# Delta rule in a two-layer trunk: decay differences by one product of masked rows, and row layouts of 1/rms by way of DRAM

## The chip, the cores and the metric

The kernel runs on one core of a Trainium2 chip. Five engines work from queues of their own: TensorE (PE: matrix products and transposes into PSUM), VectorE (DVE), ScalarE (ACT: activations, copies with scale), GpSimd (POOL) and SyncE (SP, which issues most DMAs). The metric is the device time of one execution in microseconds: the median of three runs is 2522.7 us (2521.9 to 2524.95).

## The reference

The program is a trunk of two layers over a sequence of 1024 tokens with 1024 channels. The even layer mixes a gated spatial part with a gated delta rule; the odd one is a differential attention. Each layer then has an MLP of 4096 channels and a gated embedding part (ple). Every part begins with an RMS norm, `x * rsqrt(mean(x*x) + eps) * gain`. What the change touches is the decay inside the delta rule, and the norms. Of the reference:

```
def l2_normalize(x):
    return x * lax.rsqrt(jnp.sum(x * x, axis=-1, keepdims=True) + NORM_EPS)

def chunk_gated_delta_rule(q, k, v, g, beta):
    ...
    gc = jnp.cumsum(g, axis=-1)
    causal = jnp.tril(jnp.ones((c, c), dtype=bool))
    strict = jnp.tril(jnp.ones((c, c), dtype=bool), k=-1)
    diff = gc[..., :, None] - gc[..., None, :]
    decay = jnp.where(causal, jnp.exp(jnp.where(causal, diff, 0.0)), 0.0)
    a = jnp.where(strict, jnp.einsum('bhnid,bhnjd->bhnij', k_beta, k) * decay, 0.0)
    u = solve(t_mat, v_beta)
    w = solve(t_mat, k_beta * jnp.exp(gc)[..., None])
    qk = jnp.einsum('bhnid,bhnjd->bhnij', q, k) * decay
```

For each chunk and each of four heads, `diff` is a square matrix of differences of running sums, and `decay` its masked exponential. The kernel works with eight chunks of 128 tokens (the result doesn't depend on the chunk's length).

## The kernel before

**Stages.** The tokens lie in two halves of 512. The x of the first half is loaded and transposed, then the input projection of the even layer begins, and from there on a long row of projection products fills TensorE: an fp32 value is split in a high and a low part (`hi`, `lo`, of type fp32r; ScalarE casts, VectorE subtracts), and three products with 512 columns each stand for one (`mm3`, tiles `mm`). These products are dealt out as fill: `pump(n)` emits the projection up to its unit n, and between two calls the code emits a piece of the delta rule. `FILLA` units are shared over the eight chunks' preparation, `FILLB` over the solver, `FILLC` and `FILLD` over what follows (`merge`, `prep`), `FILLS` over the eight steps of the recurrence. The class `Ordered` ties TensorE's instructions to that order with a lag of three slots; a code part in `high_priority` is put ahead of what else is ready by the scheduler that orders the other engines' queues. The times of the stages in the profile: decay and k times k of the eight chunks 100 to 141 us, the triangular solver from 147 us, its merge from 189 us, all beside projection products.

**The delta rule's preparation.** `gates()` forms the running sums of the gates for all chunks by four small products (`pg`, 128x32 for each kind), exponentiates them (`eg`), and keeps three forms of the sums: `gsum`, its negative `nsum`, and `gparts`, a high and a low part in fp32r. `spatial_weights()` transposes the spatial part's weights (`pws`). Then, for each chunk c, the generator `ahead(c)`:

- forms `pd`, the sums of the chunk laid out along the columns for each head: eight products of 128x128 (four heads, high and low part), a column of `gparts` broadcast as weights against an identity in fp32r (`identr`); `pd` lies in one of the two PSUM buffers with the tag `aux`;
- takes exponentials of 128x128 on ScalarE, head by head, with the negative or the positive sum of the row as bias: `ring` (the strict lower part, `am`) and `dec` (the causal part, `du`); POOL masks each with an `affine_select`;
- transposes k (`pk`), and gets its inverse length `rk` (`inverse_length`: a square of 512 columns on ScalarE, a reduction on VectorE, a power on POOL) and the scaled copy `kt`; the q of a chunk goes the same way in a later stage;
- multiplies k by itself (`pkk`, 128x128 for each head, fp32), also into an `aux` buffer, and VectorE multiplies it into `ring`;
- stores the diagonal blocks (`diag`) and the whole (`am_dram`) in DRAM by SP's queue.

`solve()` loads `diag` into `work` and inverts the small blocks on VectorE (the result is `dt`), and builds the larger inverse on TensorE with 32x32 pieces (`py`, `pz`).

**The row layouts of 1/rms.** `rms(half, ...)` computes 1/rms of 512 tokens as `r`, with the token along the partitions (128x4). Where a later step needs it along the columns, the same in all partitions, four products of `r`, broadcast as weights, with the identity bring it into a PSUM buffer (eight instructions in fp32, tile `aux`), and ScalarE copies it into `rb` (line 267). Nine places do this. Three of them matter here: the second half in `load_x`, the first half of the MLP's result (`take_hs(0)` in `mlp`) and the second half in `ple`, where `rms(1, sqs)` is called while the third gate product is emitted. The MLP runs twice, once per layer, and in the last layer nothing uses the rows of the first half's result.

## Time and profile before

| | |
|---|---|
| median of three runs | 2522.7 us |
| profiled execution | 2522.26 us, span 2520.5 us |
| TensorE busy | 2503.7 us (99%), granted clock 1.0 |
| VectorE, ScalarE, GpSimd busy | 1839.6 (73%), 1307.8 (52%), 258.2 us (10%) |
| DMA | 398.49 MB, mean 158 GB/s |

How to read the lines that follow. A row of a timeline has the start in us from the span's beginning, the length, the engine, the line of the kernel, the operation, the tiles it writes and reads (`out<-in`), and how many instructions it joins. Timelines and groups give an instruction's own duration, and neighbours on one engine overlap; the chain of the work that ended last gives each piece only the time by which it moves the end on (start, length, engine, tile, line). A row of the waits has engine, waiting tile and line, what it waited for, then the sum in us, the times, and the longest. A row of the windows has the window, its length, the busy time of PE, PEld (weight loads), DVE, ACT and POOL with their instructions, the granted clock, and the DMA share and rate. TensorE executes an fp32 product of small size in two passes, each of which is an instruction in the rows. A group's row has the line, the operation, shapes, the count, the busy time and the mean; a DMA's group ends with the size in KB and the median time from issue to landing.

### The profile page before, as it was taken

What the parts mean: (1) busy time and instruction counts of PE and PEld (TensorE: products, weight loads), DVE (VectorE), ACT (ScalarE), POOL (GpSimd) and SP (SyncE); (2) the same over time, 40 slices, a digit from 0 to 9 for tenths busy, and PEclk for the clock granted to TensorE, in tenths of its full rate; (3) what the DMA queues carried; (4) which work ended last, traced back from release to release, by engine and by line L of the source; (5) the groups of instructions that cost most, each with busy time, mean ns of one, the idle gap of its engine ahead of it and who ended that gap; (6) DMA issues with size and microseconds to landing.
All of it is one profiled execution on the core that took longest, in us unless ns stands there. A gap on an engine that the chain in (4) does not pass through costs nothing.

```text
span 2520.5 us, 39929 instructions
## 1 busy us (share of the span) xinstructions
PE 2503.7 (99%) x13982; PEld 2145.8 (85%) x13982; DVE 1839.6 (73%) x3664; ACT 1307.8 (52%) x2633; POOL 258.2 (10%) x227
## 2 busy tenths in 40 slices
PE   9999999999999999999999999999999999999999
PEld 7998998888888878888999999988788888888887
DVE  7868665696667787656577777786886677787586
ACT  6645473555555434544466666564654455445452
POOL 0210220000000000000433333310000000000000
PEclk9999999999999999999999999999999999999999
DMA  7464435466557756543211111147375558655651
GB/s 239 131 172 106 137 116 190 130 209 213 184 166 273 236 175 195 183 148 111 86 48 51 47 43 43 60 147 260 133 227 196 177 187 278 214 188 182 204 180 59
DMA packets 310482, 398.49 MB, mean 158 GB/s; under 512 B 43428, under 2 KB 179592, under 8 KB 310280
## 3 DMA queue, kind: packets, MB, share of 16 engines
q1 hardware_dynamic: 309720, 395.40, 49.1%
q8 instruction: 110, 1.80, 0.3%
q14 instruction: 92, 0.75, 0.1%
q10 hardware_dynamic: 560, 0.53, 0.1%
HBM read 289.40 MB, written 106.43 MB: 157 GB/s over the span
## 4 chain that ended last, share of the span: by engine, by line
PE 95%; DVE 2%; ACT 1%; DMA 1%; issue 0%; POOL 0%; ACTq 0%; DVEq 0%; POOLq 0%
PE mm L76 83%; PE po L76 3%; PE aux L76 2%; PE qk L76 2%; PE tr L79 2%; DVE lg L1020 0%; DMA guv<-uv_dram 0%; PE aux L79 0%; PE pkk L76 0%; PE pks L76 0%; PE pkq L76 0%; PE pd L76 0%; ACT t L1466 0%; DVE lg L1031 0%; ACT lg L1023 0%
## 5 line engine op out<-in xcount | busy, mean ns | idle before, releaser
L76 PE MATMUL mm<-g,w 128*128 128x512 f32 x2592 | 603.4, 394 | 1.1 <-ACT g L223 1.0
L223 ACT CAST w<-raw 128x512 fp32r<-128x512 f32 x598 | 365.7, 618 | 457.4 <-PE mm L76 388.5
L76 PEld LDWEIGHTS mm<-g,w 128*128 128x128 f32 x2592 | 486.0, 188 | 116.1 <-ACT g L223 1.4
L76 PE MATMUL mm<-hi,w 128*128 128x512 f32 x1728 | 554.0, 396 | 0.3 <-ACT hi L1230 0.3
L76 PE MATMUL mm<-w,hi 128*128 128x256 f32 (+2 forms) x2528 | 504.3, 295 | 0.0
L224 DVE TENSOR_TENSOR w<-raw,w 128x512 fp32r<-128x512 f32 x534 | 365.1, 690 | 179.9 <-ACT w L223 172.6
L76 PEld LDWEIGHTS mm<-w,hi 128*128 128x128 f32 x2528 | 400.6, 188 | 13.5
L76 PEld LDWEIGHTS mm<-hi,w 128*128 128x128 f32 x1728 | 324.2, 188 | 73.8 <-ACT hi L1230 0.7
L76 PE MATMUL mm<-w,lo 128*128 128x256 f32 (+2 forms) x1264 | 369.9, 293 | 0.0
L76 PE MATMUL mm<-lo,w 128*128 128x512 f32 x864 | 340.8, 395 | 0.9 <-DVE lo L1231 0.9
L76 PE MATMUL mm<-t,w 128*128 128x512 f32 x1152 | 270.9, 394 | 1.2 <-ACT w L223 1.2
L76 PEld LDWEIGHTS mm<-t,w 128*128 128x128 f32 x1152 | 216.2, 188 | 52.8 <-ACT w L223 1.6
L76 PEld LDWEIGHTS mm<-w,lo 128*128 128x128 f32 x1264 | 238.0, 188 | 5.3
L76 PEld LDWEIGHTS mm<-lo,w 128*128 128x128 f32 x864 | 162.4, 188 | 37.0 <-DVE lo L1231 1.4
L260 POOL TENSOR_TENSOR r<-ms,mhalf 128x4 f32<-128x4 f32 x12 | 13.3, 1109 | 1519.4 <-DVE ms L258 1492.5
L224 DVE TENSOR_TENSOR g<-graw,g 128x512 fp32r<-128x512 f32 x216 | 147.0, 684 | 8.7 <-DMA gd<-g 8.1
L223 ACT CAST g<-graw 128x512 fp32r<-128x512 f32 x216 | 132.7, 617 | 28.5 <-PE mm L76 7.7
L1023 ACT ACTIVATE lg<-lg,nm 128x128 f32<-128x128 f32 (+7 forms) x128 | 99.4, 777 | 81.9 <-DVE nm L1020 79.6
L350 ACT ACTIVATE g<-g 128x512 f32<-128x512 f32 x96 | 60.5, 631 | 116.1 <-DVE g L284 109.2
L1020 DVE CUSTOM_DVE_ANT_0 lg<-qk,al 128x512 f32<-128x512 f32 (+3 forms) x128 | 74.9, 589 | 38.7 <-PE qk L76 36.6
L224 POOL TENSOR_TENSOR w<-raw,w 128x512 fp32r<-128x512 f32 x64 | 84.2, 1339 | 111.0 <-ACT w L223 64.8
L76 PE MATMUL mm<-ohi,w 128*128 128x512 f32 x256 | 85.4, 400 | 0.6 <-ACT ohi L1077 0.4
(346 smaller groups left out, 3586.3 us busy)
## 6 DMA issues: line engine op xcount, KB each, us to landing
raw<-in_w_mlp_dram SPq DMA_DIRECT2D x352, 256.0 KB, 3.2
graw<-gd SPq DMA_DIRECT2D x224, 256.0 KB, 3.0
gd<-g SPq DMA_DIRECT2D x192, 256.0 KB, 3.2
raw<-in_w_ple_gate_dram SPq DMA_DIRECT2D x76, 256.0 KB, 3.3
acc<-h_dram SPq DMA_DIRECT2D x64, 256.0 KB, 4.6
keep<-in_w_mlp_dram SPq DMA_DIRECT2D x64, 256.0 KB, 4.2
raw<-in_w_in_e_dram SPq DMA_DIRECT2D x60, 256.0 KB, 3.8
h_dram<-acc SPq DMA_DIRECT2D x48, 256.0 KB, 3.0
```

Of the source, the lines that this page charges most:

```text
L76: self._next(self.engine.matmul(*a, **k))
L79: self._next(self.engine.transpose(*a, **k))
L223: self.nc.scalar.copy(hi, src)
L224: (lo_engine or self.nc.vector).tensor_tensor(lo, src, f32(hi), ALU.subtract)
L260: nc.gpsimd.tensor_tensor(r, ms, self.mhalf[:, 0:4], ALU.pow)
L350: nc.scalar.activation(g, src, AF.Relu)
L1020: nc.vector.tensor_tensor_reduce(out=lg[:, k0:k1], in0=ps[:, : k1 - k0], in1=al[:, u0 + k0 : u0 + k1], scale=-1.0, scalar=3.0e38 if c == 0 ...
L1023: nc.scalar.activation(lg[:, :n], lg[:, :n], AF.Exp, bias=nm[:, r, nch - 1 : nch], scale=-1.0, accum_out=me.sums[:, b, r : r + 1])
```

## The change

- `gparts`, `gsum`, `nsum` and `identr` go. In their place `gates()` puts the high and low parts of the sums side by side, transposes them once (`pgt`, 128x128), and builds two sets of rows: `own` (ones in the upper 64 rows, the sums in the lower) and `others` (the negative sums above, ones below; one copy for each head, with the rows of other heads set to zero). Both are in fp32r, in one large tile `sums`.
- For a chunk, ScalarE copies `own` with the rows of other chunks scaled to zero (a 128x128 mask copy), and a single product of 128x512 gives the differences of all four heads, `pd`, at once. The two exponentials then take 512 columns each, without a bias and with a scale of 1 and -1.
- `inverse_length` of `rk` squares head by head and lets ScalarE sum the squares (`accum_out`); VectorE's reduction stays for the other case.
- `rms` can send the rows by DRAM (`far`): a DMA writes `r` to a small DRAM tile `rd`, another broadcasts it to all partitions as `rb`. This is used in the three places named above; in the last layer's MLP the rows are not made at all.
- `gates()` is emitted with high priority, `FILLC` and `FILLD` go from 26 and 31 to 28 and 29.

```diff
-FILLA, FILLB, FILLC, FILLD = 62, 36, 26, 31
+FILLA, FILLB, FILLC, FILLD = 62, 36, 28, 29
...
-        self.identr = self.cp.tile([P, P], F32R, name="identr")
-        nc.vector.tensor_copy(self.identr, self.ident)
...
         rb = None
-        if rows:
+        if rows and far:
+            d = self.dp.tile([4, P], F32, name=self.nm("rd"))
+            nc.sync.dma_start(d.rearrange("t p -> p t"), r)
+            rb = self.sp.tile([P, HT], F32, tag=f"rb{half}", name=self.nm("rb"), bufs=1)
+            nc.sync.dma_start(rb, d.rearrange("t p -> (t p)").partition_broadcast(P))
+        elif rows:
             pb = self.aux_ps()
...
-        self.take_hs(0)
+        self.take_hs(0, rows=not last, far=True)
...
-                        rb[1] = self.rms(1, sqs)[1]
+                        rb[1] = self.rms(1, sqs, far=True)[1]
...
-            self.take_hs(half, ms)
+            self.take_hs(half, ms, far=half > 0)
...
-        gsum, nsum = carve([P, NC, G], 0), carve([P, NC, G], 0)
-        gparts = self.cp.tile([P, 2, NC, G], F32R, name="gparts")
+        in_any, in_chunk, in_head = carve([P, NC, G], 0), carve([P, NC, 1], 0), carve([P, G, 1], 0)
+        nc.vector.tensor_reduce(flat(in_any), self.ident.rearrange("p (q x) -> p x q", q=4), AX.X, ALU.add)
+        nc.vector.tensor_reduce(flat(in_chunk), in_any, AX.X, ALU.add)
+        nc.vector.tensor_reduce(flat(in_head), in_any.rearrange("p c h -> p h c"), AX.X, ALU.add)
+        own = carve([P, P], 0)
+        nc.vector.memset(own[0:64], 1.0)
...
-            nc.vector.tensor_copy(flat(gsum), pg[:, 0])
-            self.split(flat(gsum), flat(gparts[:, 0]), flat(gparts[:, 1]))
-            nc.vector.tensor_scalar(flat(nsum), pg[:, 0], -1.0, None, ALU.mult)
+            parts = self.tmp(P).rearrange("p (k q x) -> p k q x", k=2, q=2)
+            hi = hi_sums
+            nc.scalar.copy(hi, pg[:, 0])
+            for k in range(2):
+                nc.scalar.copy(parts[:, k, 0], f32(hi))
+                nc.vector.tensor_tensor(parts[:, k, 1], pg[:, 0], f32(hi), ALU.subtract)
+            pt = aux([P, P], "aux", "pgt")
+            self.pe.transpose(pt, parts.rearrange("p k q x -> p (k q x)"), self.ident)
+            nc.scalar.copy(own[64:P], pt[64:P])
+            other = self.tmp(P)
+            nc.vector.memset(other[64:P], 1.0)
+            nc.scalar.mul(other[0:64], pt[0:64], -1.0)
+            nc.vector.tensor_tensor(others, bc(other, G, 1), in_head.to_broadcast([P, G, P]), ALU.mult)
...
         def inverse_length(pt, name, sq):
-            nc.scalar.activation(sq, pt, AF.Square)
             l2 = self.sp.tile([P, G], F32, tag="l2", name=self.nm("l2"))
-            nc.vector.tensor_reduce(l2, sq, AX.X, ALU.add)
+            if name == "rk":
+                for h in range(G):
+                    nc.scalar.activation(sq[:, h], pt[:, h], AF.Square, accum_out=l2[:, h : h + 1])
+            else:
+                nc.scalar.activation(sq, pt, AF.Square)
+                nc.vector.tensor_reduce(l2, sq, AX.X, ALU.add)
...
+            w = sums[:, 1, (c % 4) * P : (c % 4 + 1) * P]
+            nc.scalar.activation(w, own, AF.Copy, scale=in_chunk[:, c])
             pd = aux([P, G, P], "aux", "pd")
-            for h in range(G):
-                for i in range(2):
-                    self.pe.matmul(pd[:, h], lhsT=gparts[:, i, c, h : h + 1].to_broadcast([P, P]), rhs=self.identr, start=i == 0, stop=i == 1)
-            for own, other in ((gsum, 1), (nsum, -1)):
+            self.pe.matmul(flat(pd), lhsT=w, rhs=flat(others), start=True, stop=True)
+            for other in (1, -1):
                 e = ring[:, c % 4] if other > 0 else self.slot(("c2", "c3", "c6", "d0")[c % 4], [P, G, P], F32, "dec")
-                for h in range(G):
-                    nc.scalar.activation(e[:, h], pd[:, h], AF.Exp, scale=-float(other), bias=own[:, c, h : h + 1])
+                nc.scalar.activation(e, pd, AF.Exp, scale=float(other))
...
-        gates()
+        sums = self.slot("A3", [P, 2, HT], F32R, "sums")
+        others = sums[:, 0].rearrange("p (h t) -> p h t", h=G)
+        with self.tc.high_priority(EARLY):
+            gates()
```

More of the change, by code (lines that the diff above doesn't have):

```diff
@@ L243, in add_square, with take_hs, rms @@
             nc.vector.tensor_tensor(self.sqs[half], self.sqs[half], sq, ALU.add)
-    def take_hs(self, half, ms=None, rows=True):
-        self.r[half], self.rb[half] = self.rms(half, self.sqs[half], ms, rows)
+    def take_hs(self, half, ms=None, rows=True, far=False):
+        self.r[half], self.rb[half] = self.rms(half, self.sqs[half], ms, rows, far)
         self.hs[half] = self.hs_new[half]
-    def rms(self, half, sqs, ms=None, rows=True):
+    def rms(self, half, sqs, ms=None, rows=True, far=False):
         nc = self.nc
@@ L1295, in even_mix @@
         nc.vector.memset(state, 0.0)
+        hi_sums = self.cp.tile([P, NC * G], F32R, name="hi_sums")
         def gates():
```

## The prediction

> **What bounds the kernel now.** I read the page first: the busy shares, the slices and the chain that ended last.
>
> ```profile
> span 2520.5 us, 39929 instructions
> PE 2503.7 (99%) x13982; PEld 2145.8 (85%) x13982; DVE 1839.6 (73%) x3664; ACT 1307.8 (52%) x2633; POOL 258.2 (10%) x227
> PEclk9999999999999999999999999999999999999999
> PE 95%; DVE 2%; ACT 1%; DMA 1%; issue 0%; POOL 0%; ACTq 0%; DVEq 0%; POOLq 0%
> ```
>
> TensorE is busy 99% of the span and is 95% of the chain, at its full clock in every slice. The waits say how much of the rest is waiting; their first row is the largest:
>
> ```profile
> PE tr L79 <- DVE olo L1078: 2.3, 3, 1.2
> ```
>
> So a TensorE instruction taken out shortens the program by its own length, as long as no new wait appears. Where one could, the share of VectorE matters, so I took the windows of the stretch in which the decay work runs (in each: PE, PEld, DVE, ACT, POOL):
>
> ```profile
> 100.00:120.00 20.00, 20.00 (x127) 17.61 (x126) 18.73 (x52) 13.61 (x42) 9.32 (x12) 1.00 0.51 158
> 120.00:140.00 20.00, 20.00 (x141) 18.42 (x140) 18.96 (x54) 13.72 (x42) 7.88 (x11) 1.00 0.68 190
> ```
>
> Here VectorE is at 94 to 95% and ScalarE at 68%: TensorE bounds, with VectorE just behind. The chain in this window (98 to 142 us) is TensorE alone, and its pieces give the advance per instruction without overlap:
>
> ```profile
> by line: PE mm L76 62.2%; PE pkk L76 16.9%; PE pd L76 15.1%; PE pk L79 6.0%
> ...
> 99.84 0.76 PE pk L79 x7
> ...
> 102.32 1.51 PE pd L76 x14
> 103.83 2.13 PE mm L76 x9
> ```
>
> pd is 15.1% of 44 us, 6.6 us for 64 instructions (0.108 each by the x14 row). A 128x512 product takes 2.13 / 9 = 0.237 us, a transpose 0.76 / 7 = 0.109 us.
>
> **The change, part by part.** (a) Eight products of 128x512 replace the 64: 8 x 0.237 = 1.9 us for 6.6, a gain of 4.7 us. (b) The row layout of 1/rms goes by DRAM in three places, and is dropped in one where nothing reads it.
>
> ```profile
> 61.02 0.89 PE aux L76 x8
> ...
> L76 PE MATMUL aux<-ident,r x72: 270/275/275, 23.7 to 2363.8; 128*128 128x128 f32 x72
> ```
>
> The 72 instructions are nine places of eight, and four of them go: 4 x 0.89 = 3.6 us of TensorE, with four ScalarE copies. (c) One transpose (pgt) is new: +0.1 us. (d) What TensorE now meets at the first chunks. On TensorE, where chunk 0 and 1 start (pd: decay differences, pkk: k times k, mm: input projection), before:
>
> ```order
> L76 MATMUL pd_1143<-identr,gparts 128x128 x7
> L76 MATMUL pd_1213<-identr,gparts 128x128 x7
> L76 MATMUL mm_1268<-hi_177,w_1129 128x512
> ...
> L76 MATMUL mm_1268<-hi_201,w_1190 128x512
> L79 MATMUL pk_1461<-ident,qkv_692 128x128
> L79 MATMUL pk_1540<-ident,qkv_692 128x128
> L76 MATMUL pkk_1254<-qkv_277 128x128 x4
> ```
>
> and after:
>
> ```order
> L76 MATMUL mm_1257<-hi_199,w_1189 128x512
> L76 MATMUL pd_1153<-sums_1046 128x512
> L76 MATMUL pd_1213<-sums_1046 128x512
> L79 MATMUL pk_1418<-ident,qkv_691 128x128
> L79 MATMUL pk_1487<-ident,qkv_691 128x128
> L76 MATMUL pkk_1243<-qkv_279 128x128 x4
> ```
>
> Nine projection products stood between the second pd and pkk; now none does. pkk takes the PSUM buffer of the first pd (two buffers turn), so it waits until both exponentials of chunk 0 are done. On ScalarE, for the same place, after (own and the other rows from pgt, then masks, squares, tanh, convolution copy, exponentials):
>
> ```order
> L1334 COPY carved_239<-pgt_1069 64x128
> L1337 ACTIVATE t_1072<-pgt_1069 64x128
> L1600 ACTIVATE sums_1046<-carved_239 128x128 x3
> L1580 ACTIVATE sq_1290,l_254_1291<-pk_1285 128x128 x4
> L1600 ACTIVATE sums_1046<-carved_239 128x128
> L1580 ACTIVATE sq_1359,l_266_1360<-pk_1354 128x128 x4
> L1386 ACTIVATE t_1129<-t_1124 128x512
> L1382 ACTIVATE t_1204<-cx_1201,cols 128x512
> L1605 ACTIVATE ring_1151<-pd_1153 128x512
> L1605 ACTIVATE dec_1157<-pd_1153 128x512
> ```
>
> All of these come after pgt and ahead of the release; before, only two squares of 128x512 stood between the tanh and the exponentials. Their prices (ScalarE, timelines):
>
> ```profile
> 103.09 1.14 ACT L1580 ACTIVATE ring<-pd,carved 128x128 f32<-128x128 f32 x4 [1.48 <-PE pd L76]
> 104.11 1.16 ACT L1580 ACTIVATE dec<-pd,carved 128x128 f32<-128x128 f32 x4
> ...
> 107.11 0.74 ACT L1365 ACTIVATE t<-t 128x512 f32<-128x512 f32 x1
> 107.64 0.83 ACT L1361 ACTIVATE t<-cx,cols 128x512 f32<-128x512 f32 x1
> ...
> 321.10 1.28 ACT L1797 ACTIVATE qkv<-qkv,fo 128x128 f32<-128x128 f32 x4 [2.87 <-DVE fo L1795]
> ...
> 323.29 0.40 ACT L1466 ACTIVATE t<-guv,mean 128x128 f32<-128x128 f32 x1
> 323.58 0.20 ACT L1466 ACTIVATION_READ_ACCUMULATOR t<-guv,mean 128x1 f32 x1
> 323.67 0.39 ACT L1466 ACTIVATE t<-guv,mean 128x128 f32<-128x128 f32 x1
> ```
>
> Back to back, a 128x128 exponential from PSUM advances (104.11 - 103.09) / 4 = 0.255 us, a scaled copy in SBUF 1.28 / 4 = 0.32, a 128x512 activation 0.53 (107.11 to 107.64), a summed square 0.38 with its read of the sum (323.29 to 323.67). That last one reads SBUF and has a pointer bias, which the new squares from PSUM have not; so they lie between 0.255, as if the sum were free, and 0.38. I take 0.28, nearer the exponential's row, since that reads PSUM too. The chain on ScalarE: two rows out of PSUM 0.5 (0.255 each at most), four masks 1.2 (the first is only part of a row ahead), eight squares 2.2, tanh 0.53, convolution copy 0.6, two exponentials 1.1: 6.1 us, with ends of 5.9 and 6.9. TensorE has, from pgt to pkk, 11 transposes (1.2), ten products (2.4), two pd (0.5) and two pk (0.2): 4.3 us. pkk therefore waits 6.1 + 0.3 for two handovers between engines (an estimate from the pd pieces: 102.32 + 1.51 ends where the next begins, so the trace shows none here; ends 0 and 0.6) - 4.3 = 2.1 us, within 1.6 and 3.2. pk_1418 waits for the tanh of the same row of work and lies inside that wait.
>
> The Trainium skill ("ScalarE: Activation LUTs", What ACT_TABLE_LOAD costs) says that every [128,1] pointer operand adds about 93 ns to an ACTIVATE. By that rule the summed square without its bias would be an estimated 0.38 - 0.093 = 0.29 us, and the wait about the same as mine; by the L1466 row as it stands it would be 0.8 us longer. No row here shows the same square with and without a pointer.
>
> (e) VectorE loses the reduction of rk (one of 128x512 per chunk) and gains a few in the idle start; ScalarE per chunk stays about equal: eight exponentials at 0.255 (2.0) and one square of 512 (0.5) become two of 0.53, four summed squares (1.1) and a mask (0.3), 2.5 against 2.5. So the later chunks cost nothing new; if that cover fails it is the third rival. The solver behind has room:
>
> ```profile
> 183.35 2.07 DVE L1647 STREAM_TRANSPOSE dt<-work 128x1024 f32<-128x1024 f32 x1
> ...
> 189.28 2.21 PE L76 MATMUL py<-dt,ay 32*32 32x32 f32 x128
> ```
>
> TensorE starts py 3.9 us after its input is there. It comes 0.9 (b) + 4.7 - 0.1 - 2.1 = 3.4 us earlier there, so even an unmoved solver would be in time by 0.5 us; the two fill units moved across it take nothing from the sum. (f) The DMA pairs: r is there (POOL) long before the rows are first read (DVE), and short transfers land within 5 us:
>
> ```profile
> 29.25 1.45 POOL L260 TENSOR_TENSOR r<-ms,mhalf 128x4 f32<-128x4 f32 x1 [7.82 <-DVE ms L841]
> 62.82 0.68 DVE L1357 TENSOR_TENSOR cx<-mm,rb 128x512 f32<-128x512 f32 x1
> ...
> 1025.01 1.01 POOL L260 TENSOR_TENSOR r<-ms,mhalf 128x4 f32<-128x4 f32 x1 [540.55 <-DVE ms L258]
> 1113.05 0.68 DVE L591 TENSOR_TENSOR t<-mm,rb 128x512 f32<-128x512 f32 x1
> ...
> 1120.47 1.01 POOL L260 TENSOR_TENSOR r<-ms,mhalf 128x4 f32<-128x4 f32 x1 [92.39 <-DVE ms L258]
> 1165.83 0.69 DVE L591 TENSOR_TENSOR t<-mm,rb 128x512 f32<-128x512 f32 x1 [0.23 <-PE mm L76]
> ...
> kg<-in_attn_k_gain_dram SPq DMA_DIRECT2D x2, 0.2 KB, 3.1
> ...
> vg<-in_gmlp_v_gain_dram SPq DMA_DIRECT2D x2, 256.0 KB, 3.9
> ```
>
> kg is 64 elements of four bytes, vg a row broadcast to all partitions: 3.1 + 3.9 = 7 us against 32, 87 and 44. In the first place SP issues other loads up to about 42 us, and the pair stands among them:
>
> ```profile
> 36.54 0.48 SPq L854 DMA_DIRECT2D kg<-in_attn_k_gain_dram  x1
> 41.91 0.97 SPq L101 DMA_DIRECT2D raw<-in_w_in_e_dram  x2
> ```
>
> The store of r comes right behind the first row and the broadcast ahead of the second, so it lands near 46, still 17 us early. What the pairs hold is SP's queue, where the broadcast waits for the store to land and later loads stand behind it. In the second place:
>
> ```profile
> 1025.12 0.43 SPq L324 DMA_DIRECT2D raw<-in_w_mlp_dram  x1
> 1029.25 0.32 SPq L324 DMA_DIRECT2D graw<-gd  x1
> ...
> 1038.08 0.62 ACT L223 CAST g<-graw 128x512 fp32r<-128x512 f32 x1
> ```
>
> SP idles from 1025.6 to 1029.25, about as long as r (1026.0) and kg's 3.1 us need; and with four buffers turning, the load of 1029.25 is read by the fourth cast after it, at 1038.08, landing (three us) some 5.8 us ahead. Cost 0.
>
> Sum: -4.7 - 3.6 + 0.1 + 2.1 = -6.1 us. The profiled execution took 2522.26 us (span 2520.5 and 1.8 around it), 0.4 under the median of 2522.7; so 2516.2 by its own time, 2516.6 by the median. I say 2516.8, for a few tenths of handovers.
>
> **Rivals.** A, likeliest: as summed, the wait between 1.6 and 3.2: 2515.9 to 2517.8. B, no wait: ScalarE's squares slip ahead of pgt, or the exponentials come in time: -8.2, 2514.5. For it: 99% busy; against it: the order above. C, the stretch from 99 to 140 turns into VectorE's and ScalarE's: VectorE is at 95% there, and chunks pass the same two buffers each time. TensorE's saving in it beyond the first two chunks is 6 x (0.84 - 0.24) = 3.6 us; it can give all of that back, plus up to 3 more if the solver ends as much later against its 0.5 us of room: 2518 to 2523. D, the slower one: SP. If a landing went by the number of elements, r's 512 would take 8 x 3.1 = 24.8 us, and the load behind it would come 21 us late at 1029; beyond 5.8 us of room TensorE stands for 15 us, net +9, 2532. It decides from 12 us of lateness on. Against it: vg moves 256 KB in 3.9. E, the clock: after a wait TensorE could be granted less.
>
> ```profile
> 0.00:4.00 4.00, 2.58 (x12) 2.53 (x12) 0.88 (x7) 1.49 (x2) 0.69 (x6) 1.00 0.53 107
> 4.00:8.00 4.00, 2.60 (x11) 1.59 (x10) 0.77 (x2) 1.26 (x3) 0.00 (x0) 1.00 0.99 325
> ```
>
> With idle gaps of 1.4 us in each of these the clock stays 1.00. If a longer wait halved it, the 15 products behind would take 0.47 instead of 0.237, +3.5 us: 2520.2. The Trainium skill ("TensorE: Matmul & The Clock Gate", What's actually happening) has such a rule: an idle window of about 3.4 us brings the array to half its clock until a busy one of that length has passed. By that rule the wait forecast here stays under the limit; its upper end is near it.
>
> **Chances.** A 0.50, B 0.10, C 0.26, D 0.08, E 0.06. A difference of 0.2% (5.0 us) is about the least that a measurement can tell here; faster means under 2517.7: A but for its upper end and B, 0.56; slower is D with the worst of C, 0.12; the rest, most of C and E, 0.32. The range leaves out D, the worst of C and the fastest of B: 2514.2 to 2521.8.
>
> **What would show it.** Eight pd of 128x512 near 0.24 us and 40 instead of 72 aux<-ident,r; one row in the waits, PE pkk or pk for ACT or DVE, of about 2 us near 104; full clock behind it; rb landing within 8 us of r. Wrong would make it: further pkk, pd or py rows in the waits (C), TensorE waiting for casts near 1035 or 1130 (D), or a pd row far above 0.24.

## The result: slower, and where the time went

The changed kernel takes 2531.8 us (seven runs, 2528.7 to 2533.7), the kernel before 2522.7 beside it: a ratio of 1.0031, with a 95% interval of 1.0020 to 1.0043. It is slower by 9.1 us, where 6.1 less were forecast. The profiled execution took 2533.74 us, at the upper end of its runs. From its page:

```profile
span 2532.0 us, 39755 instructions
PE 2499.9 (99%) x13895; PEld 2139.2 (84%) x13895; DVE 1838.6 (73%) x3660; ACT 1302.2 (51%) x2649; POOL 260.0 (10%) x227
PE 88%; DVE 4%; DMA 4%; ACT 2%; issue 1%; SPq 0%; POOL 0%; DVEq 0%; ACTq 0%; POOLq 0%
```

TensorE has 3.8 us less to do than before (2503.7), but its share of the chain falls from 95 to 88%: the chain now runs through DMAs and VectorE. The waits of TensorE in the changed kernel (before, the largest was 2.3 us in three pieces):

```profile
PE aux L79 <- DVE xt L815: 5.9, 1, 5.9
...
PE mm L76 <- DVE acc L288: 2.3, 2, 2.0
...
PE pk L79 <- DVE qkv L1387: 1.8, 1, 1.8
...
PE mm L76 <- DVE w L222: 1.7, 2, 1.5
PE mm L76 <- DVE t L1186: 1.6, 1, 1.6
...
PE py L76 <- DVE xts L1719: 1.3, 2, 1.1
```

The wait of 1.8 at `pk` is the one that was forecast. The first row is the large one, and it isn't in the decay part: it is a transposition of x (`aux`, line 79), which waits for VectorE to empty a PSUM buffer (`xt`). How it comes about is read from two queues. SyncE's timeline around the first of the three row layouts, changed kernel:

```profile
38.16 0.53 SPq L263 DMA_DIRECT2D rd<-r  x1
...
42.09 0.34 SPq L861 DMA_DIRECT2D sg<-in_attn_sub_gain_dram  x1
...
47.31 0.33 SPq L265 DMA_DIRECT2D rb<-rd  x1
```

The broadcast `rb` waits for the store `rd` to land: 47.31 - 38.16 = 9.1 us. Between them stands the load of `sg`, 128 single elements that only the attention of the second layer uses, more than 1000 us later. VectorE's timeline, changed kernel:

```profile
42.78 0.68 DVE L815 COPY xt<-aux 128x512 f32<-128x512 f32 x1
52.03 0.15 DVE L862 TENSOR_SCALAR sg<-sg 128x1 f32<-128x1 f32 x1 [8.57 <-DMA sg<-in_attn_sub_gain_dram]
...
53.42 0.68 DVE L815 COPY xt<-aux 128x512 f32<-128x512 f32 x1
```

and the same place in the kernel before:

```profile
41.68 0.15 DVE L858 TENSOR_SCALAR sg<-sg 128x1 f32<-128x1 f32 x1 [0.61 <-DMA sg<-in_attn_sub_gain_dram]
...
42.41 0.68 DVE L811 COPY xt<-aux 128x512 f32<-128x512 f32 x1
```

VectorE stood 0.61 us for `sg` before and stands 8.57 now. It takes its instructions in order, so the copies of x behind it are late by as much, and TensorE with them. Windows of the changed kernel (the last two numbers of a row are the DMA share and GB/s, the one ahead of them is the granted clock):

```profile
44.00:48.00 4.00, 4.00 (x21) 3.21 (x19) 0.00 (x0) 0.00 (x0) 0.00 (x0) 1.00 0.46 28
48.00:52.00 4.00, 0.32 (x2) 0.00 (x0) 0.00 (x0) 0.00 (x0) 0.00 (x0) 0.93 0.90 287
52.00:55.00 3.00, 0.75 (x5) 0.78 (x5) 2.97 (x7) 1.82 (x3) 0.00 (x0) 0.50 0.89 309
55.00:58.00 3.00, 3.00 (x10) 2.48 (x9) 2.96 (x6) 0.42 (x1) 0.00 (x0) 0.50 0.27 95
```

While the store is out, the other transfers crawl: 28 GB/s from 44 to 48 us. SyncE's queue stands from 43.5 to 47.3 us, until the store has landed, but that isn't all: transfers that it had issued from 39.4 to 43.0 us were out already, and those whose landing the trace gives took 10.0 to 10.6 us (`sg` 9.9 by VectorE's row, where the kernel before has 2.8). The stores of x, over the whole of the kernel before and then from 36 to 54 us in the changed one:

```profile
h_dram<-xt SPq DMA_DIRECT2D x16, 256.0 KB, 5.2
```

```profile
h_dram<-xt SPq DMA_DIRECT2D x3, 256.0 KB, 10.4
```

From 48 to 54 TensorE stands, and behind that it has half its clock until 58 us. That is rival E's clock, after another wait than the one it was priced for: 10 matmuls in the last 3 us, where 17 were done in the same window before:

```profile
55.00:58.00 3.00, 3.00 (x17) 2.54 (x16) 3.00 (x7) 2.49 (x6) 0.00 (x0) 1.00 0.08 14
```

How far TensorE stood behind the kernel before, place by place, worked out from the starts of the same instructions in the timelines (place named by its time before; the last column is the kernel of the first experiment, which has no far rows at the first place):

```
us before, what starts there            changed kernel   first place on TensorE
  45.6  third transposition of x            +0.7              +1.5
  55.4  fourth, its last instruction        +8.9              +1.5
  93.1  gates (pg)                          +8.3              +1.8
 189.3  solver (py)                         +6.4              -0.1
 203.4  merge (py of xts)                   +9.0              +1.3
 244.4  recurrence                          +7.8              +0.4
 307.4  recurrence                          +9.5              +0.7
1269.3  attention                           +7.1              -1.7
1751.8  output projection                   +8.9              -1.9
2256.3  MLP of the last layer              +12.5              -1.3
2516.4  end                                +11.5              -2.3
```

8.2 us are lost between the third and the fourth transposition (0.7 of them are three projection products that moved ahead of the fourth). From gates to solver 1.9 are gained, by the two other row layouts some 2.4 (9.5 to 7.1), by the dropped one 0.9. The four later waits take 1.3 (merge; the rest of that step is moved fill work, which the other kernel has too and gets back by 244), 1.7 (305), 1.8 (1745) and 3.6 (2237 us, with a halved clock). Profiles differ from that of the kernel before by up to 1.8 us at the start already, by when x arrives, so these columns are good to about that; totals are taken from medians.

### The profile page after: what moved, and what is told of

It reads as the page before. It is cut to its first block, busy times and chain, and to the rows that moved or that the text cites. A ratio compares the mean times of both kernels' runs of the same rounds, so it can differ in the third digit from the quotient of the medians.

```text
span 2532.0 us, 39755 instructions
## 1 busy us (share of the span) xinstructions
PE 2499.9 (99%) x13895; PEld 2139.2 (84%) x13895; DVE 1838.6 (73%) x3660; ACT 1302.2 (51%) x2649; POOL 260.0 (10%) x227
## 4 chain that ended last, share of the span: by engine, by line
PE 88%; DVE 4%; DMA 4%; ACT 2%; issue 1%; SPq 0%; POOL 0%; DVEq 0%; ACTq 0%; POOLq 0%
PE mm L76 77%; PE po L76 3%; PE qk L76 2%; PE aux L76 2%; PE tr L79 2%; DMA raw<-in_w_mlp_dram 1%; DMA guv<-uv_dram 1%; DVE t L1384 0%; DVE lg L1024 0%; DMA t<-h_dram 0%; DMA raw<-in_w_in_e_dram 0%; DMA sg<-in_attn_sub_gain_dram 0%; DVE w L222 0%; ACT junk L820 0%; PE pks L76 0%
```

## Experiments

Each time stands beside runs of the kernel before on the same chip. Two theories were tested first. S: the store of `r` at the first place is the loss, by the stand for `sg`. Rival C of the prediction: the decay part gives back what it gains and takes more.

**The first place back on TensorE.** Everything else of the change stays.

```diff
-            self.take_hs(half, ms, far=half > 0)
+            self.take_hs(half, ms)
```

> The changed kernel, with the row layout of load_x (the second half of x) back on TensorE; all else as changed. Theory 1 (the store of 512 four-byte elements holds the DMA rings for 8 to 9 us at 38 to 47 us; VectorE's queue stands at sg, whose load is behind it, TensorE stands 5.9 us and then runs at half its clock): the 8.2 us that TensorE lost between 45 and 58 us come back, less 0.9 for the eight products, so 2531.8 - 7.3 = 2524.5 us, and no wait above 2.5 us before 60 us. Theory 2 (the decay part's early reductions and the gates' priority make VectorE late at the start): the wait stays, 2532.7 us.

2520.97 us against 2522.42, ratio 0.9991 (0.9982 to 1.0000); 10.8 under the changed kernel's median. The 5.9 us row is gone, and so is the half clock from 52 to 58. The first two waits of this kernel:

```profile
PE tr L79 <- DVE olo L1082: 2.3, 3, 1.2
PE pk L79 <- DVE qkv L1387: 1.8, 1, 1.8
```

**The first place alone, in the kernel before.** `far` as in the change, used in `load_x` only.

> The kernel before, with the row layout of load_x (second half) by DRAM and nothing else changed. Theory 1: the same stand near 48 to 54 us and half a clock behind it, 2522.7 + 8.2 - 0.9 = 2530.0 us. Theory 2: 2522.7 - 0.9 = 2521.8 us.

2531.1 against 2522.4: 1.0032 (1.0019 to 1.0045), the loss of the whole change. Its waits have the same row, `sg` landed as late (VectorE stood 9.67 us), and the merge has its wait too:

```profile
PE aux L79 <- DVE xt L816: 5.7, 1, 5.7
...
PE py L76 <- issue: 1.8, 1, 1.8
```

So this line of the change, without any of the decay part, gives the result. That S is the cause of the loss and C isn't follows from these two runs together.

**All rows on TensorE; the decay part by itself.** The first is the kernel above with the other two far places back as well (the dropped rows stay dropped); the second has the old fill units (26, 31) and all rows, so it is the decay part alone.

> The changed kernel with all three row layouts back on TensorE; the one that nothing reads stays dropped, and the decay part is as changed. If the pairs in the MLP and in the ple part cost nothing but save their products (theory 1): 1.8 us above the kernel with only load_x back, 2526.3 us. If their stores cost time elsewhere too (a load that comes late in the MLP or the ple part): equal to it or below, 2522 to 2524.5 us.

> The decay part alone: all row layouts as before the change, the unused one too, FILLC and FILLD at 26 and 31. By the prediction's sum (a, c, d): 2522.5 - 4.7 + 0.1 + 2.1 = 2520.0 us. By the traces so far (a gain of 1.9 us from the gates to the solver): 2520.6 us. If the waits it sets off later eat it: 2522 to 2524 us.

2523.94 against 2522.42 (1.0004, 0.9995 to 1.0013), and 2523.34 against 2522.9 (1.0001, 0.9992 to 1.0010). By the first the second and third place are worth 3.0 us (2523.94 - 2520.97; forecast 1.8), but not all of that is their products: its profile has a wait of 2.2 us for `guv` near 387 us with a window at half clock behind it (388.8 to 392.2), where the kernel with only the first place back waits 0.9 at full clock. The second says that the decay part gains nothing that can be measured, where 2.5 were forecast. In its own stretch the gain is there; from the timeline of the decay part alone, first `pg` and first `py`, and the `pg` of the kernel before:

```profile
95.10 0.97 PE L76 MATMUL pg<-carved,carved 128*128 128x32 f32 x8
189.46 2.21 PE L76 MATMUL py<-dt,ay 32*32 32x32 f32 x128
```

```profile
93.06 0.97 PE L76 MATMUL pg<-carved,carved 128*128 128x32 f32 x8
```

Before it is 189.28 - 93.06 = 96.22 us from one to the other, now 94.36: 1.9 less. Up to 386 us the gain shrinks to 1.0 (a wait of 1.0 for `guv`, 0.6 before), and by 2256 us to 0.3, with a wait for `g` that the kernel before doesn't have (1.2 at 2230 in its own time).

**The rows part without the first place.** The kernel before with the second and third place far and the dropped rows.

```diff
-        self.take_hs(0)
+        self.take_hs(0, rows=not last, far=True)
...
-                        rb[1] = self.rms(1, sqs)[1]
+                        rb[1] = self.rms(1, sqs, far=True)[1]
```

> The kernel before with the row layouts of the MLP and the ple part by DRAM and the unused one dropped; load_x on TensorE, the decay part as before. If TensorE's saving there is whole (3 x 0.89 us) and the decay part is worth little once its waits are counted: 2522.5 - 2.7 = 2519.8 us, as fast as the kernel with the decay part and old fills (2520.2). If the decay part is worth its forecast 2.5 us beyond this: that kernel stays faster by 2 us, and this one stands at 2522 us.

2520.45 against 2522.9: 0.9991 (0.9982 to 1.0000), 2.45 us less; three times 0.89 is 2.7. Here the stores land just as slowly (9.1 us at 1025) and nobody waits for them.

**Is `sg` the only link?** In the changed kernel VectorE's instruction on `sg` is emitted at the start of the attention instead of the start of the program; the store stays as slow.

```diff
-        nc.vector.tensor_scalar(sg, sg, 1.0 - lam_init, None, ALU.mult)
...
+        self.pe.behind(nc.vector.tensor_scalar(self.sg, self.sg, self.sub, None, ALU.mult), self.pe.mark)
```

> The changed kernel (store of 512 elements in load_x kept), but VectorE's scaling of sg is issued only ahead of the attention, so that nothing on VectorE waits for sg at the start; its load stays where it is. Theory 1a (the slow load of sg, in order on VectorE, is the only link from the store to TensorE): no stand near 50 us, full clock, 2531.8 - 8.2 = 2523.6 us or a little less. Theory 1b (stores of x tiles and weight loads behind the slow store hold TensorE as well): a wait of 2 to 5 us stays between 45 and 60 us, 2527 to 2530 us.

2523.45 against 2523.5 (0.9998, 0.9989 to 1.0007). Its windows:

```profile
44.00:48.00 4.00, 4.00 (x23) 3.32 (x22) 3.96 (x9) 1.23 (x3) 0.00 (x0) 1.00 0.44 61
48.00:52.00 4.00, 4.00 (x20) 3.23 (x18) 2.84 (x7) 2.02 (x4) 0.00 (x0) 1.00 1.08 378
```

The transfers crawl as before (61 GB/s), `rb` is again issued 8.5 us behind `rd`, but TensorE works on at full clock. It lacks 1.8 us to the first experiment (0.9998 against 0.9991, intervals that overlap). Its profile, 2526.66 us and the slowest of its eleven runs, keeps the changed kernel's waits at the merge (1.3), at 1745 us (1.8, with a window at half clock behind it) and 2237 us (1.8). How much of the 1.8 each of them makes isn't shown.

**Another shape of the store.** `r` is first transposed on TensorE (one instruction), and four rows of 512 bytes are stored.

```diff
-            nc.sync.dma_start(d.rearrange("t p -> p t"), r)
+            pr = self.aux_ps()
+            self.pe.transpose(pr[0:4, 0:P], r, self.ident)
+            r4 = self.tmp(P)[0:4]
+            nc.scalar.copy(r4, pr[0:4, 0:P])
+            nc.sync.dma_start(d, r4)
```

> The changed kernel, but 1/rms is transposed to four rows on TensorE (one transpose of 128x4, a ScalarE copy) before the store, which then writes four rows of 512 bytes in place of 512 elements of four. Theory 1 (the elements' size is what holds the rings): the store lands within 3 to 4 us in place of 8 to 9, no stand near 50 us, 2531.8 - 8.2 + 0.3 = 2523.9 us. Theory 3 (any pair of a store and a broadcast at that place holds the loads of the start): 2529 to 2532 us.

2521.4 against 2522.4 (0.9996, 0.9987 to 1.0005): the broadcast follows the store by 2.3 us, with no stand and at full clock. But the extra transposition comes late in TensorE's order (the pair is issued at 61.8 and 64.1), so this run changes the time of the store as well as its shape, and VectorE waits 2.1 us for `rb`.

**One square of 512 columns for `rk`**, with VectorE's reduction, as before the change (from the first experiment's kernel), and **the old fill units** (26, 31) in the same kernel.

> load_x back on TensorE, and the square of rk once more as one of 512 columns with a reduction on VectorE, as before the change. If the wait of 1.8 us ahead of the first pkk is ScalarE's chain (prediction's step d): the chain is 1.2 us shorter (8 x 0.27 against 2 x 0.5), the wait falls to 0.6 us, and the time is 1 us under that of load_x alone, 2520.0 us, if VectorE has room for eight reductions of 0.6 us; if it has none, 1 to 3 us above it, 2522 to 2524 us, with waits at pkk for VectorE.

> load_x back on TensorE, FILLC and FILLD at their old values 26 and 31. If the two moved units matter: the small waits at py near 204 us (0.3 us) come or go, within 1 us of load_x alone, 2520 to 2522 us. If they were what carries the solver's lateness, py waits over 1.4 us and the time is 2522.5 us.

2520.52 (0.9989, 0.9980 to 0.9998) and 2520.19 (0.9985, 0.9976 to 0.9994) against 2523.5. With one square ScalarE's chain is shorter, and TensorE's first wait falls from 1.8 to 0.6 (at `pkk`, for the exponentials); but later `pkk` wait longer in its place, and `guv` is later:

```profile
PE pgm L76 <- DVE guv L1513: 2.0, 1, 2.0
PE pkk L76 <- ACT dec L1600: 1.8, 2, 1.2
```

With the old fills TensorE is 0.5 us earlier by the recurrence (in the first experiment the gain of 1.9 before the solver is 1.3 there, with the old fills 1.8). It is the fastest version with the decay part, 0.15% under the kernel before.

**How long does such a store take?** Two first attempts put scratch stores, which nothing reads, beside the gate products of `ple` and into the attention; nothing of the computation is left out.

> load_x back on TensorE, and three more stores of 1/rms to scratch in the ple part that nothing reads: 128, 256 and 512 elements of four bytes (one, two and four columns). If the time to landing goes with the elements: some 3.5, 5.3 and 8.8 us. If it is a fixed time of such a store, or came from other traffic: the three are alike, 2.5 to 4 us on a queue with little in it.

> load_x back on TensorE, and eight small stores to scratch that nothing reads, in the attention, where the DMA is busy 1 to 19% only: twice each of 128, 256 and 512 elements of four bytes, and of 128 runs of 16 bytes (the same 512 numbers in another layout). If landing goes with the number of separate elements: about 3.5, 5, 8.8 us, and 3.5 us for the runs of 16 bytes. If it goes with the bytes or is fixed: the last two are alike.

Neither tells number from kind. In the first, 128, 256 and 512 elements landed in 10.2, 17.3 and 17.7 us, but behind up to a megabyte of loads, and the third 2.4 us behind the second; in the second all in 9.2 to 10.7, while stores of 256 KB beside them took 10.5. The times of the kernels are 2519.14 and 2521.31, one run each. So four more kernels put one store each into the two places of the rows part (1025 and 1121 us, the rows themselves on TensorE), and read it back by a small transfer that waits for its landing. Each ran once, for its trace (2521.72 to 2524.42 us beside 2523.96 of the kernel before).

```diff
+            if kind == "col":
+                src, d = r[:, 0:1], self.dp.tile([P, 1], F32, name=self.nm("dosecol"))
+            elif kind == "run":
+                src, d = r, self.dp.tile([P, 4], F32, name=self.nm("doserun"))
+            elif kind == "few":
+                src, d = r[0:16, 0:1], self.dp.tile([16, 1], F32, name=self.nm("dosefew"))
+            else:
+                src, d = r, self.dp.tile([4, P], F32, name=self.nm("doseall")).rearrange("t p -> p t")
+            nc.sync.dma_start(d, src)
+            one = self.sp.tile([1, 4], F32, tag="doseback", name=self.nm("doseback"), bufs=2)
+            nc.sync.dma_start(one[:, 0 : d.shape[1]], d[0:1])
```

> The kernel before with a scratch store in each of the two quiet places where the rows were sent by DRAM (1025 and about 1121 us), read back by one small transfer that waits for its landing; the rows themselves stay on TensorE and nothing of the computation is left out. Here: 128 elements of four bytes at the first place, 128 runs of 16 bytes at the second. From issue to the issue of the reading: if the landing goes by the number of elements (512 took 8.4 to 9.1 us), the 128 elements take 2 to 3.5 us and the 128 runs the same; if it goes by the size of each piece and not their count, the 128 elements take 8 to 9.5 us and the runs of 16 bytes also more than 6; if scattered single elements alone are slow, 8 to 9.5 and about 3.

> The same with the two places exchanged: 128 runs of 16 bytes at 1025 us, 128 elements of four bytes at 1121. What is a property of the place keeps its landing, what is one of the store moves with it.

> The same with 16 elements of four bytes, from 16 partitions, at both places. By the number of elements 1.5 to 2.5 us from issue to the issue of the reading; if there is a fixed time for stores of single elements, 7 to 9.5 us.

> The same with all 512 elements of four bytes at both places: the scale for the three others. 8.4 to 9.5 us in both places by every theory.

SyncE's timelines at the first place, one fence for each kernel (128 elements; 128 runs of 16 bytes; 16 elements; 512 elements):

```profile
1027.86 0.32 SPq L272 DMA_DIRECT2D dosecol<-r  x1
1036.48 0.25 SPq L274 DMA_DIRECT2D doseback<-dosecol  x1
```

```profile
1027.05 0.32 SPq L272 DMA_DIRECT2D doserun<-r  x1
1030.57 0.25 SPq L274 DMA_DIRECT2D doseback<-doserun  x1
```

```profile
1027.68 0.33 SPq L272 DMA_DIRECT2D dosefew<-r  x1
1030.43 0.24 SPq L274 DMA_DIRECT2D doseback<-dosefew  x1
```

```profile
1027.61 0.37 SPq L272 DMA_DIRECT2D doseall<-r  x1
1037.10 0.67 SPq L274 DMA_DIRECT2D doseback<-doseall  x1
```

From issue to the issue of the reading, in us (the second column from the same rows at the second place):

```
store                      1025 us   1121 us
16 elements of 4 bytes       2.8       1.3
128 elements                 8.6       8.0
512 elements                 9.5      10.2
128 runs of 16 bytes         3.5       1.4
```

The place matters by some 2 us at most, and the count past 128 little: four times as many elements take 0.9 to 2.2 us more. 128 pieces of 16 bytes take a sixth to two fifths of 128 pieces of four. What is slow is a store of single elements, with a step somewhere between 16 and 128 of them that these runs don't place. They don't separate the size of the pieces from their crowding either: 128 pieces of four bytes fill 512 bytes of DRAM, 128 of sixteen fill 2048. The Trainium skill ("DMA: Bandwidth & Descriptors", Specifications) gives 512 bytes as the size below which a transfer is done by read-modify-write. Both kinds here are below it, and they differ by 5 to 6.6 us, so that line by itself does not tell them apart. The windows of the kernel with 512 elements before and during the store:

```profile
1024.00:1028.00 4.00, 4.00 (x23) 3.41 (x22) 2.46 (x5) 1.16 (x3) 1.42 (x2) 1.00 0.89 272
1030.00:1036.00 6.00, 6.00 (x28) 4.85 (x27) 3.38 (x6) 2.28 (x4) 0.00 (x0) 1.00 0.33 21
```

272 GB/s fall to 21. Unlike at 42 us this isn't the store alone: SyncE, which waits to issue the reading, issued nothing from 1028.5 to 1037.1, so that one load of 256 KB (1028.03) was all that stood beside the store. TensorE doesn't notice in this place.

**The change with the store mended.** All three far places stay; `r` is stored as it lies, in 128 runs of 16 bytes, the broadcast keeps that order, and VectorE reads `rb` by a view with a step of four. In the second of the two the fill units are the old ones.

```diff
-            d = self.dp.tile([4, P], F32, name=self.nm("rd"))
-            nc.sync.dma_start(d.rearrange("t p -> p t"), r)
+            d = self.dp.tile([P, 4], F32, name=self.nm("rd"))
+            nc.sync.dma_start(d, r)
...
-            nc.sync.dma_start(rb, d.rearrange("t p -> (t p)").partition_broadcast(P))
+            nc.sync.dma_start(rb, d.rearrange("p t -> (p t)").partition_broadcast(P))
+            rb = rb.rearrange("q (p t) -> q t p", t=4)
```

> The changed kernel, all three far places kept, but r stored as it lies (128 runs of 16 bytes) and the columns put in order by the reader's view on VectorE. If the loss at the first place comes from the landing of the store of single elements: rb issued 1.4 to 4 us behind rd at all three places, no stand of TensorE near 48 to 54 us, full clock there, and 2520.1 (the kernel with the first place on TensorE less 0.9), 2519 to 2522. If the far way is bad at the first place whatever its store (its broadcast among the loads of x, the scheduler's order of VectorE at the merge), 2524 to 2530.

> The same with the two fill units back (26, 31). By the sum of what the single runs showed 2519.5: 2520.2 with the old fills and the first place on TensorE, less 0.9 for its eight products, plus the 0.2 to 1.3 that the merge's order of VectorE costs where the first place is far. If the far way costs at the first place whatever its store, 2524 or more.

2523.63 and 2524.42 against 2522.63: 1.0003 (0.9994 to 1.0013) and 1.0007 (0.9998 to 1.0016). The median store lands in 2.3 us (the broadcast of the first place is issued 5.4 and 5.3 us behind its store, where 1.4 to 4 were expected, with other issues in between), and the window from 48 to 52 us is whole again in the first of the two:

```profile
rd<-r SPq DMA_DIRECT2D x3, 2.0 KB, 2.3
...
48.00:52.00 4.00, 4.00 (x22) 3.30 (x21) 3.96 (x9) 2.88 (x5) 0.00 (x0) 1.00 0.37 138
```

So the shape of the store alone takes the loss away; its medians were expected at 2519 to 2522, though, and 2519.5. Part of what is left stands at the merge, in the waits of the first and of the second:

```profile
PE py L76 <- DVE xts L1725: 1.4, 2, 1.1
```

```profile
PE py L76 <- DVE xts L1725: 2.7, 2, 2.5
```

These waits come in each kernel whose first place is far, and in none whose first place is on TensorE: the far rows give the scheduler another order, and in it VectorE's copies `xts` stand behind operations of the projection (`t<-cx`). In the second kernel the wait is followed by a window at half clock (204.9 to 208.3 us), about 1.7 us more. Another part may be the price of the view: with its step of four, VectorE's product with `rb` takes 1.07 us in place of 0.68, in 28 products, and the waits at `pkk` for VectorE's `ring` are 1.3 us, where the changed kernel has 0.6. Together this gives back more than the eight products of that place save; no run takes the parts asunder.

**The changed kernel once more**, in another batch, for the size of the loss.

> The changed kernel once more, for a second trace. The stand of 5.9 us near 50 us and the half clock behind it must be there again. The waits near 211, 305, 1745 and 2237 us (1.1, 1.5, 1.6 and 2.0 us, the last with half a clock) recur if they follow from the order of the queues, and vary by over 0.5 us if they follow from the DMA's timing in one execution. 2529 to 2534 us.

2528.45 against 2522.9: 1.0023 (1.0013 to 1.0033), 5.5 us. Its profile has the same stand (5.7 us at the transposition) and shorter late waits (1.3 at 1745 and 1.6 at 2237, no half clock behind the latter).

## Why the prediction was wrong, step by step

By runs of one part each, against the terms of the sum:

```
part                                forecast    measured (medians, us)
decay part alone                      -2.5        +0.4   (-2.0 to +2.5)
second, third place, dropped rows     -2.7        -2.5   (-4.5 to  0.0)
first place                           -0.9        +8.7   (+4.8 to +11.4)
whole change                          -6.1        +9.1, +5.5 in the second batch
```

**(f), the DMA pairs at "Cost 0", is the step that failed.** It took the landing of the store from `kg`, 3.1 us. That row is a load of 64 elements; the store of 512 took 8.8 at the third place, where the trace gives it, and 9.1 to the broadcast's issue at the first. The prediction asked who reads `rb`, and there it was right: `rb` was in time in every place of the changed kernel, though its sign "`rb` landing within 8 us of `r`" failed (issued 8.5 to 9.1 us behind the store). It asked what stands behind the pair in SyncE's queue at the second place; at the first it said that the pair stands among other loads, and priced none of them. At 42 us one of these was `sg`, whose reader stands in VectorE's order ahead of the copies of x. One more row, VectorE's on `sg` with its 0.61 us wait, would have shown that there was no room at all.

**Rival D** had the sign, and the wrong mechanism. It said that a landing by the number of elements (24.8 us) would hold SyncE's queue and so a load of weights near 1029, and that it decides from 12 us of lateness. The landing doesn't go by the number, it stayed under 12 us, and at 1029 TensorE worked on. What the queue held at the first place cost nothing either, as the run with `sg` moved away shows.

**(a)** held but for 0.4 us. From the changed kernel, `pd` and the products that were left of the row layouts:

```profile
L76 PE MATMUL pd<-sums x8: 388/397/482, 112.2 to 141.0; 128*128 128x512 f32 x8
...
L76 PE MATMUL aux<-ident,r x40: 270/275/275, 24.6 to 1805.8; 128*128 128x128 f32 x40
```

By the starts of their neighbours, and without the waits between, the eight instructions advance TensorE by 2.6 us and the 64 of before by 7.0: 4.3 less, where 4.7 were forecast (1.9 for 6.6). The forecast 0.237 us is what one takes in a row of its like (0.235 from the first to the second `pd`); ahead of `pkk` three take 0.32 to 0.35, and where a wait follows it is 0.39 to 0.40. A row's duration (397 ns) isn't that advance, since it holds the overlap with the next.

**(b)** held for the count, 40 instead of 72, and for two places and the dropped one; at the first, (f) took it back many times over.

**(c) and (d)** held in size. The wait was 1.8 us (forecast 2.1, within 1.6 and 3.2), but before `pk` and not `pkk`: it ended with VectorE's `qkv`, behind ScalarE's tanh, at 108.08 us in the first experiment. The exponentials that were to end it end 0.14 us later, while `pk` still ran, so `pkk` met no wait of its own. That the two end so close together is nothing that the prediction worked out. With one square, where `pk` doesn't wait, `pkk` does (0.6 us). ScalarE's chain, from the timeline of the first experiment:

```profile
102.37 0.26 ACT L1334 COPY carved<-pgt 64x128 f32<-64x128 f32 x1 [3.08 <-PE pgt L79]
...
103.70 0.26 ACT L1580 ACTIVATE sq<-pk 128x128 f32<-128x128 f32 x1
103.86 0.20 ACT L1580 ACTIVATION_READ_ACCUMULATOR sq<-pk 128x1 f32 x1
103.95 0.26 ACT L1580 ACTIVATE sq<-pk 128x128 f32<-128x128 f32 x1
...
107.61 0.61 ACT L1605 ACTIVATE dec<-pd 128x512 f32<-128x512 f32 x1
```

It takes 108.22 - 102.37 = 5.85 us, forecast 6.1. A summed square advances by 103.95 - 103.70 = 0.25, its lower bound: the read of the sum costs no time of its own there. The Trainium skill's 93 ns for a pointer operand ("ScalarE: Activation LUTs", What ACT_TABLE_LOAD costs) gave an estimate of 0.29, nearer than the 0.38 of the row with a pointer, and still above.

**(e)** was wrong in small things: a second wait came at `pkk` for VectorE's product with `ring`, 0.6 us, so the stretch gave 1.9 and not 2.5 (4.3 - 0.1 - 1.8 - 0.6 = 1.8). Rival C was right about the place. In the changed kernel the chain from 98 to 142 us, all TensorE before, has these shares:

```profile
by line: PE mm L76 27.6%; DVE t L1384 18.0%; DVE ring L1631 13.7%; DVE kt L1617 6.6%; issue 5.6%; DVE qkv L1387 5.5%; DVE cx L1378 4.5%; DVE sc L1622 3.8%; DVE sc L1621 3.1%; PE pk L79 2.0%; PE pg L76 1.8%; DVE w L222 1.5%; ACT t L1386 1.5%
```

so VectorE carries it, and by this chain a further saving on TensorE there would be worth nothing (no run tried one). The two moved fill units cost about 0.5 us by the recurrence, where nothing was counted. Why the 1.9 us are not in the end time of the decay part alone stays open: late waits took most of it in the one profile, and with an interval of 4.5 us the medians can't tell this from the smaller gains of the forecast's range.

**Rival E**: the clock did halve, at a price of about 2 us at the first place (half clock from 54.25, when TensorE began again, to 58.24). The Trainium skill ("TensorE: Matmul & The Clock Gate", What's actually happening) puts it down to an idle window of some 3.4 us on a free-running grid. The stand from 48.3 to 54.2 nearly fills the window ahead of the half clock (it began at 51.4, and TensorE was busy for 0.3 us of the 3.4 before), so here rule and trace are close.

## What to carry to other kernels

A DMA that stores single elements across partitions is no short transfer: price it by a store of the same piece size, and store runs of at least 16 bytes, leaving the order to the reader, whose view with a step has a price too (here 0.4 us for each of VectorE's products). Who waits for the new transfer's result is only half of the question; the other half is which loads fly beside it, and what stands behind their readers on an in-order engine. A product taken off TensorE is worth its length only where no other engine is as near to the end, and a change far from a place can reorder that place through the scheduler.

## What the runs showed of the hardware that was not expected

Stores of single four-byte elements to DRAM took 8.0 to 10.2 us for 128 as for 512, and transfers issued up to 5 us behind one landed in 9.9 to 10.6 us, where the kernel before has medians of 2.8 to 5.2. And the clock was halved after waits shorter than an idle window. In the changed kernel a wait of 2.0 us for `acc` near 2237 is followed by one window at half clock:

```profile
2236.00:2239.36 3.36, 1.40 (x7) 0.86 (x6) 2.44 (x5) 1.14 (x2) 0.00 (x0) 1.00 0.45 150
2239.36:2242.77 3.41, 3.41 (x9) 2.63 (x10) 3.41 (x7) 0.00 (x0) 0.00 (x0) 0.50 0.36 114
2242.77:2246.00 3.23, 3.23 (x16) 2.61 (x15) 3.23 (x6) 0.00 (x0) 0.00 (x0) 1.00 0.88 283
```

TensorE was busy for 1.4 us of the window ahead, and lost half of the next, about 1.7 us. The same followed the waits of 2.2 and 2.0 us for `guv` in two experiments (all rows on TensorE, one square), one of 2.5 at the merge (runs of 16 bytes, old fills) and one of 1.8 at 1738 us (`sg` later). The length of the half-clock window, 3.41 us, agrees with the Trainium skill ("TensorE: Matmul & The Clock Gate", What's actually happening); that a whole window must be idle does not. A wait of 1.8 us near 105 brought none in any run, though it left TensorE busy for 1.6 us of such a window in the first experiment, as much as the one at 1738 us did. So the length of a wait doesn't decide it, and these runs don't show what does.
